# Two more 8 KB buffers for expert weights in a two-layer transformer block, and four kinds of small DMAs moved from GpSimd's queue to ScalarE's

## The chip, the cores and the metric

The kernel runs on one core of one Trainium2 chip. Its engines are TensorE (PE, with its weight loads as PEld), VectorE (DVE), ScalarE (ACT), GpSimd (POOL) and SyncE (SP); here SP does nothing but start DMAs, and ACT and POOL start a few as well. The metric is the device time of one execution in microseconds (us).

## The reference, cut to what matters

Two layers work on 256 latent tokens and 256 context tokens of 1024 features, all in float32. Each layer has a dense part and a mixture of experts. The second layer updates the latent tokens alone.

```python
for l in range(DEPTH):                                    # DEPTH = 2, last = (l == 1)
    mod_x = silu(c) @ w_mod[l] + b_mod[l]                 # six vectors: shift, scale and gate, twice
    mod_c = silu(c_ctx) @ w_mod[l] + b_mod[l]
    p_x = modulate(rmsnorm(x, norm1_g[l]), sh1, sc1) @ w_in[l]
    p_c = modulate(rmsnorm(ctx, norm1_g[l]), csh1, csc1) @ w_in[l]
    # attention, convolution and pooling branches, gated, merged, times w_out
    x = x + g1 * merge_branches(attn_x, conv_x, pool_x, gate_x, lp)
    if not last:
        ctx = ctx + cg1 * merge_branches(attn_c, conv_c, pool_c, gate_c, lp)
    x = x + g2 * expert_choice_ffn(modulate(rmsnorm(x, norm2_g[l]), sh2, sc2), ...)
    if not last:
        ctx = ctx + cg2 * expert_choice_ffn(modulate(rmsnorm(ctx, norm2_g[l]), csh2, csc2), ...)
return rmsnorm(x, final_norm_g)

def expert_choice_ffn(h, w_router, w_gate, w_up, w_down): # 16 experts, each takes its top 32 tokens
    aff = softmax(h @ w_router)
    g, idx = top_k(aff.T, 32)
    a, u = h[idx] @ w_gate[e], h[idx] @ w_up[e]           # w_gate, w_up, w_down: 1024 x 1024 per expert
    y[idx] += ((silu(a) * u) @ w_down[e]) * g
```

The three weight matrices of an expert have 4 MB each, so the experts of one layer read 192 MB, and of both layers 384 MB of the 530 MB that the kernel moves.

## The kernel before, in words

**Stages.** For each layer l the program runs through: the first norm with its modulation; the products for q, k and v; attention; the convolution and pooling branches; the merge of the branches; the output projection (`project`) with the router and its top 32 (`route`); the gather of the chosen tokens (`gather`); and a loop over 16 experts. Layer 0 works on both streams together (512 columns), layer 1 on the latent stream. In an expert, L1079 is the gate and up product, L1084 and L1086 the activation, L1094 the transposes, L1103 (layer 0) and L1108 (layer 1) the down product; L1115 and L1118 multiply by the gate, and after every fourth expert of layer 0, every second of layer 1, L1125 and L1128 add the group's result to the tokens.

**The dense weights.** w_mod, w_in and the like come in pieces of 512 KB or 1 MB into a ring of five buffers "w" of 8 KB per partition. SP starts these loads (L198, L363, L390, L728) in the order of the program, and each waits until the buffer that it is given is free.

**The start.** Nothing of layer 0 can begin before its first shift and scale are known. `mod_first` computes them in two halves of four feature blocks; each half takes eight loads of 512 KB from w_mod (L363), four buffers with two loads each, and multiplies them by the conditioning vectors (L367). Its bias is read from the small tiles mbias at L373. The four copies that fill mbias (L421: 64 partitions by 256, in which one row of b_mod is repeated over 32 partitions) are started by POOL before the change. Between the two halves SP starts two loads of w_in for q (L390). The transposes of the normed tokens (L404) and the first q products (L479, L480) stand between the halves on PE.

**The expert weights.** Each expert takes twelve loads of 1 MB: four pairs of gate and up, and four of down. `prefetch(n)` starts the next n loads on SP (L334), and `slot` says into which buffer each goes: it goes round a list, `order`, which names all buffers that are free by the time of the experts. In layer 0 the list has 15 entries (x0 to x3, the ring's five, two each of B and ws, A0, A1), and "y" once; in layer 1 it has 19. `eload` hands out a prefetched buffer and starts a new load where there is none. A load whose buffer is still read waits at the head of SP's queue, and everything behind it waits too.

**Small copies.** ACT already starts the biases of the later modulation products (modb, L227), the router's weights (rt, L839) and w_pool. Before the last expert POOL starts a copy of one row, final_norm_g (L1058), which PE spreads over the partitions (L1061).

**How order is made.** Each engine runs its instructions in the order that the program gives it, and waits on semaphores. DMAs started by SP or ACT use eight semaphores in turn, in the order of the program, over both queues; such a DMA waits until the one eight places before it has landed. DMAs started by POOL have semaphores of their own. DMAs that POOL starts have their descriptors built in on-chip memory, for which 16 KB per partition are set aside.

Of the kernel before, what the change touches and what calls it, by code (L numbers as in the profile page):

```python
# [10 lines left out]
F32 = mybir.dt.float32  # L11
# [7 lines left out]
DM, SEQ, CTX, DEPTH = 1024, 256, 256, 2  # L19
# [4 lines left out]
EPS = 1e-6  # L24
# per layer: conv taps issued per step of a section; engine of the low part of a split (v: DVE, p: GpSimd);
# engine that scales a head's probabilities; units per chunk of the modulation products
TAPS = dict(attn=(1, 4), pool=(4, 0), merge0=(8, 1), merge2=(9, 18))
# [11 lines left out]
def const_tables():  # L39
    """Tables that depend on shapes alone."""  # L40
    f = np.float32
    kc = np.zeros((128, KC_END), f)
    p = np.arange(128)
    kc[:, KC_ID:KC_ID + 128] = np.eye(128, dtype=f)
    kc[p ^ 16, KC_PERM + p] = 1.0
    kc[:, KC_U:KC_U + 128] = (p[:, None] <= p[None, :])
    kc[:, KC_MA:KC_MA + 128] = np.where(p[None, :] > p[:, None], f(-1e30), f(0))
    kc[:, KC_MB:KC_MB + 128] = np.where(p[None, :] < p[:, None], f(-1e30), f(0))
    kc[:, KC_IOTA:KC_IOTA + 32] = np.arange(1, 33)
    kc[:, KC_SCOL] = p % 32 + 1  # L50
    t = np.arange(SEQ)
    for g, w in enumerate(POOLW):
        cnt = np.clip(t + w - w // 2, 0, SEQ) - np.clip(t - w // 2, 0, SEQ)
        r = (f(w) / cnt.astype(f)).astype(f)
        kc[:, KC_EDGE + 16 * g:KC_EDGE + 16 * g + 8] = r[:8]
        kc[:, KC_EDGE + 16 * g + 8:KC_EDGE + 16 * g + 16] = r[-8:]
    row, col = (t // 64).astype(f), (t % 64).astype(f)
    fr = (f(10000.0) ** (-np.arange(16, dtype=f) / f(16))).astype(f)
    rope = np.zeros((128, 2, SEQ), f)
    for q in range(128):  # L60
        d = q % 64
        ang = (row if d < 32 else col) * fr[d % 16]
        sgn = f(-1.0) if (d // 16) % 2 == 0 else f(1.0)
        rope[q, 0] = np.cos(ang)
        rope[q, 1] = sgn * np.sin(ang)
    return kc, rope.reshape(128, 2 * SEQ)
# [3 lines left out]
def dit_block(ctx: ExitStack, tc: tile.TileContext, out, kc_in, rope_in, x, c, ctx_in, c_ctx,  # L70
# [3 lines left out]
    nc = tc.nc  # L74
# [9 lines left out]
    RB = 5  # L84
# [24 lines left out]

# [1 line left out]
    gps = open_psum("psd0", mm=3, md=1, ax=4)  # L111
# [11 lines left out]
    kt = misc[:, 512:512 + KC_END - KC_U]  # L123
# [7 lines left out]
    VN1, VN2, VCB, VLG, VLB, VPS = 0, 16, 32, 40, 48, 56  # L131
    nc.gpsimd.dma_start(kt, kc_in[:, KC_U:KC_END])

# [45 lines left out]
    def rms_scale(ss, n):  # L179
        """(ss / DM + EPS) ** -0.5"""  # L180
        r = small([128, 2], "rstd")
        nc.gpsimd.tensor_scalar(r[:, :n], ss[:, :n], 1.0 / DM, EPS, op0=ALU.mult, op1=ALU.add)
        nc.gpsimd.tensor_tensor(r[:, :n], r[:, :n], nhalf[:, :n], op=ALU.pow)
        return r

    for l in range(DEPTH):
        last = l == DEPTH - 1
        NS = 1 if last else 2
        N = 256 * NS

        # ================= dense part =================
        if l:
# [95 lines left out]

# [1 line left out]
        order = ["x0", "x1", "x2", "x3"]  # L290
        if last:
            order = ["xc", "A1"] + order + ["x4"] + ["w"] * RB + ["B", "B", "A0", "D", "D", "ws", "ws"]
        else:
            order += ["w"] * RB + ["B", "B", "A0", "A1", "ws", "ws"]
# [3 lines left out]
        def slot(name):  # L298
            if once and nload[0] == 4:
                tag = once.popleft()  # L300
            else:
                tag = order[nload[0] % len(order)]
                nload[0] += 1
            if tag == "w":
                return ring(name)
            if tag == "ws":
                return L.tile([128, 2048], F32, tag="ws", name=name, bufs=2)
            if tag == "xc":
                return P0.tile([128, 2048], F32, tag=tag, name=name)
            if tag[0] == "A":  # L310
                return half(tag, name)
            if tag in "BD":
                if tag in pair:
                    return pair.pop(tag)[:, 2048:]
                pair[tag] = big(tag, name)
                return pair[tag][:, :2048]
            return MO.tile([128, 2048], F32, tag=tag, name=name)
# [23 lines left out]

# [1 line left out]
        xn = [half(f"A{s}", "xn").rearrange("p (t d) -> p t d", t=2) for s in range(2)]  # L343
# [12 lines left out]
        def mod_first(hf, tag):  # L356
            """shift and scale of the first norm, feature blocks 4 hf .. 4 hf + 3"""
            ps = bank(tag)
# [57 lines left out]
        if l == 0:  # L416
            mbias = [t2("mbias", 256) for _ in range(2)]
            for f in range(2):
                for a in range(2):
                    o = 1024 * a + 512 * f  # L420
                    nc.gpsimd.dma_start(  # L421
                        mbias[f][64 * a:64 * a + 64], b_mod[0, o:o + 512].rearrange(
                            "(g n) -> g n", g=2).unsqueeze(1).to_broadcast([2, 32, 256]))
            first = mod_first(0, "md")
            next(first)
            small_operands()
            next(first, None)
            qw = [qload(0)]
            for d in range(4):
                modulated(d, (0, 1))  # L430
            for _ in mod_first(1, "ax"):
                pass
        else:
            qw = [qload(0)]
# [4 lines left out]
        def pump_mod(n=1):  # L439
            """advance the remaining modulation products by n chunks"""  # L440
            while n > 0:
                if cur_mod[0] is None:
                    if not bg:
                        return
                    cur_mod[0] = mod_group(*bg.popleft())
                if next(cur_mod[0], "end") == "end":
                    cur_mod[0] = None
                else:
                    n -= 1
# [25 lines left out]
        def mm3(ps, w, a, nk, n):  # L475
            """ps += w.T @ a over nk chunks of 128, each operand in two exact parts"""
            (wh, wl), (ah, al) = w, a
# [19 lines left out]

# [1 line left out]
        QS = DR.tile([128, NH, 256], F32R, tag="qf", name="QS")  # L499
# [17 lines left out]
        for u in range(2):  # L517
            tv = qw.pop() if qw else qload(u)
            for v in range(2):
# [5 lines left out]
                if NS == 2:  # L525
                    nc.scalar.activation(qx[:, 256:512], ps[:, 256:512], AF.Copy)
                # each head's rows: the leading part, and the rest on the other 64 partitions
                for kv in range(2):
# [28 lines left out]

# [1 line left out]
        def branch(name):  # L559
# [41 lines left out]
        def weigh(s, kv, pT, pr4, rs):  # L601
            """normalised probabilities, keys on the partitions"""
            nk = 4 if s == 0 else 2
# [31 lines left out]

# [1 line left out]
        W = 256 + 2 * CPAD  # L637
# [41 lines left out]

        if last:  # L680
            prefetch(2)

# [1 line left out]
        wp = DR.tile([128, 4, 128], F32, tag="k2", name="wp")  # L684
# [32 lines left out]

# [1 line left out]
        m = [half(f"A{i}", "m") for i in range(NS)]  # L719
# [46 lines left out]
        for g in range(4):  # L766
# [6 lines left out]
                                           op1=ALU.subtract)  # L773
# [1 line left out]
        def conv_norm():  # L775
# [51 lines left out]

        # ================= output projection, router, top-k =================
        tail[0] = True
# [55 lines left out]
        def route(s):  # L885
# [53 lines left out]
            wk = t2("wk", 256)  # L939
            m8 = MO.tile([48, 8], F32, tag="m8", name="m8", bufs=2)  # L940
            cur = pa[0:NE, 0:256]
# [36 lines left out]

# [1 line left out]
        def gather(s, parts):  # L980
# [17 lines left out]

        prefetch(2)
        rt = route(0)  # L1000
# [26 lines left out]

        # ================= experts =================
        GE = 4 if NS == 2 else 2
        REP = 128 // GE  # L1030
        nsq = [small([128, 2, 2], "nsq") for _ in range(NS)]
        for e in range(NE):
# [3 lines left out]
            if e % GE == GE - 1:  # L1036
                # scatter matrices of the group: (expert, slot) by token, scaled by the affinity
                sgs = []
# [16 lines left out]
            if last and e == NE - 1:  # L1055
                fgt, res = slot("fg"), slot("xo").rearrange("p (t d) -> p t d", t=2)
                frow, fg = fgt[0:1, 1024:2048], [fgt[:, 512 * h:512 * h + 512] for h in range(2)]
                nc.gpsimd.dma_start(frow, final_norm_g.unsqueeze(0))  # L1058
                for h in range(2):
# [4 lines left out]

            # gate and up: column tiles of the array side by side
            nb = 2 if NS == 2 else 1
# [136 lines left out]
```

## Time and profile before

| what | value |
|---|---|
| time, median of 3 runs (lowest to highest) | 1769.62 us (1764.06 to 1772.02) |
| span of the profiled execution, first to last instruction | 1765.2 us |
| mean granted TensorE clock | 0.953 of full speed |
| busy: PE, DVE, ACT, POOL | 87%, 38%, 23%, 13% |
| moved by DMA | 529.94 MB, mean 300 GB/s |
| layer 0: dense part and router, experts | 0 to 531 us, 531 to 1012 us |
| layer 1: dense part and router, experts and final norm | 1012 to 1297 us, 1297 to 1765 us |

The profiled execution has no time of its own on record besides its span, so sums are made against the span; the median of the three runs lies 4.4 us above it, which stands for what a run takes around its first and last instruction and for the scatter between runs. The busy shares are means over stages with different limits. In a stage in which the DMA engines move 409 GB/s all the time, PE's share says nothing about what bounds it; where PE is busy all the time and the DMA engines rest, the reverse holds.

### The profile page before, as it was taken

What the parts mean: (1) busy time and instruction counts of PE and PEld (TensorE: products, weight loads), DVE (VectorE), ACT (ScalarE), POOL (GpSimd) and SP (SyncE); (2) the same over time, 40 slices, a digit from 0 to 9 for tenths busy, and PEclk for the clock granted to TensorE, in tenths of its full rate; (3) what the DMA queues carried; (4) which work ended last, traced back from release to release, by engine and by line L of the source; (5) the groups of instructions that cost most, each with busy time, mean ns of one, the idle gap of its engine ahead of it and who ended that gap; (6) DMA issues with size and microseconds to landing.
All of it is one profiled execution on the core that took longest, in us unless ns stands there. A gap on an engine that the chain in (4) does not pass through costs nothing.

```text
span 1765.2 us, 19600 instructions
## 1 busy us (share of the span) xinstructions
PE 1537.8 (87%) x7792; PEld 809.1 (46%) x7792; DVE 668.7 (38%) x1144; ACT 407.7 (23%) x760; POOL 236.1 (13%) x242
## 2 busy tenths in 40 slices
PE   5999989999989999898899899999978766667676
PEld 2665566888654433232333267789742111111111
DVE  2568993452551221121211278965532110111011
ACT  2455312232431100000000157434421000000001
POOL 1300430154730000000000020225100000000000
PEclk9999999999999999999999999999989888888888
DMA  9733536254638999999999845666799999999996
GB/s 307 270 126 127 166 108 232 78 180 146 218 120 334 409 409 409 408 409 409 409 409 409 319 178 173 215 232 207 297 364 409 409 409 409 409 409 409 409 409 248
DMA packets 184331, 529.94 MB, mean 300 GB/s; under 512 B 11768, under 2 KB 60352, under 8 KB 179120
## 3 DMA queue, kind: packets, MB, share of 16 engines
q1 hardware_dynamic: 179472, 526.25, 78.4%
q10 hardware_dynamic: 4096, 1.97, 0.4%
q8 instruction: 61, 1.00, 0.2%
q0 software_dynamic: 672, 0.47, 0.1%
q14 instruction: 30, 0.25, 0.0%
HBM read 527.60 MB, written 1.05 MB: 299 GB/s over the span
## 4 chain that ended last, share of the span: by engine, by line
PE 37%; DMA 27%; DVE 5%; ACT 2%; POOL 2%; issue 1%; SPq 0%; POOLq 0%; ACTq 0%; DVEq 0%
DMA we<-in_w_e_up_dram 22%; PE mm L1079 11%; PE mm L1103 5%; DMA we<-in_w_e_down_dram 3%; PE mm L1108 3%; PE mm L480 2%; PE mm L988 2%; PE mm L479 2%; PE mm L482 2%; PE ax L1125 2%; PE mm L873 2%; DMA rt<-in_w_router_dram 1%; DVE hm L1086 1%; DVE acc L461 1%; PE ax L1094 1%
## 5 line engine op out<-in xcount | busy, mean ns | idle before, releaser
L1079 PE MATMUL mm<-we,xeT 128*64 128x512 f32 (+1 forms) x2048 | 445.9, 656 | 95.6 <-DMA we<-in_w_e_up_dram 75.3
L1079 PEld LDWEIGHTS mm<-we,xeT 128*64 128x64 f32 (+1 forms) x2048 | 126.6, 129 | 405.6 <-issue 201.1
L479 PE MATMUL mm<-hh,ws 128*128 128x512 f32 (+1 forms) x672 | 223.3, 351 | 1.4 <-ACT hh L413 1.2
L480 PE MATMUL mm<-hl,ws 128*128 128x512 f32 (+1 forms) x672 | 220.8, 347 | 0.0
L1086 DVE TENSOR_TENSOR hm<-si,mm 64x512 f32<-64x512 f32 x48 | 33.1, 690 | 468.1 <-ACT si L1084 467.2
L212 ACT ACTIVATE ws<-w 128x1024 fp32r<-128x1024 f32 x132 | 139.1, 1057 | 273.3 <-PE mm L482 186.2
L1084 ACT ACTIVATE si<-mm 64x512 f32<-64x512 f32 x48 | 28.4, 591 | 751.1 <-PE mm L1079 751.1
L461 DVE SCALAR_TENSOR_TENSOR acc<-up,dw,acc 128x512 f32<-128x512 f32 (+1 forms) x240 | 154.5, 687 | 0.9
L213 DVE TENSOR_TENSOR ws<-w,ws 128x1024 fp32r<-128x1024 f32 x94 | 123.6, 1319 | 71.9 <-ACT ws L212 71.5
L479 PEld LDWEIGHTS mm<-hh,ws 128*128 128x128 f32 x672 | 129.1, 193 | 31.5 <-issue 10.7
L480 PEld LDWEIGHTS mm<-hl,ws 128*128 128x128 f32 x672 | 129.2, 193 | 18.1 <-DVE hl L414 2.4
L1103 PE MATMUL mm<-we,hT 128*64 128x512 f32 x512 | 128.8, 635 | 8.4 <-ACT hT L1098 8.4
L482 PE MATMUL mm<-hh,ws 128*128 128x512 f32 (+1 forms) x672 | 134.8, 341 | 0.5 <-DVE ws L213 0.4
L213 POOL TENSOR_TENSOR ws<-w,ws 128x1024 fp32r<-128x1024 f32 x38 | 96.2, 2537 | 213.4 <-ACT ws L212 177.5
L482 PEld LDWEIGHTS mm<-hh,ws 128*128 128x128 f32 x672 | 107.6, 190 | 17.7 <-issue 2.4
L1044 POOL COPY sg<-kc 48x128 f32<-48x128 f32 (+1 forms) x16 | 4.4, 286 | 774.6 <-PE ax L1125 773.5
L1108 PE MATMUL mm<-we,hT 128*32 128x512 f32 x512 | 87.5, 790 | 11.9 <-DMA we<-in_w_e_down_dram 8.2
L1115 DVE TENSOR_TENSOR Y<-mm,G 32x512 f32<-32x512 f32 x64 | 44.0, 687 | 138.5 <-PE mm L1103 137.8
L1103 PEld LDWEIGHTS mm<-we,hT 128*64 128x64 f32 x512 | 39.2, 145 | 88.5 <-issue 75.1
L1125 PE MATMUL ax<-Y,sg 128*128 128x512 f32 x128 | 60.6, 619 | 8.8 <-DVE Y L1118 6.4
L1118 DVE TENSOR_TENSOR Y<-mm,G 64x512 f32<-64x512 f32 x32 | 22.0, 689 | 91.9 <-PE mm L1108 91.5
L749 POOL TENSOR_TENSOR m<-m,th 128x512 f32<-128x512 f32 (+1 forms) x32 | 36.6, 1143 | 145.1 <-DVE th L747 145.0
(271 smaller groups left out, 1594.6 us busy)
## 6 DMA issues: line engine op xcount, KB each, us to landing
we<-in_w_e_gate_dram SPq DMA_DIRECT2D x128, 1024.0 KB, 18.2
we<-in_w_e_up_dram SPq DMA_DIRECT2D x128, 1024.0 KB, 18.3
we<-in_w_e_down_dram SPq DMA_DIRECT2D x128, 1024.0 KB, 18.3
w<-in_w_mod_dram SPq DMA_DIRECT2D x40, 1024.0 KB, 5.0
w<-in_w_in_dram SPq DMA_DIRECT2D x38, 1024.0 KB, 5.2
w<-in_w_out_dram SPq DMA_DIRECT2D x12, 1024.0 KB, 5.1
w<-in_w_mod_dram SPq DMA_DIRECT2D x16, 512.0 KB, 10.8
w<-in_w_in_dram SPq DMA_DIRECT2D x8, 512.0 KB, 12.1
```

The source lines that it names most:

```text
L212: nc.scalar.activation(h, src, AF.Copy)
L213: (nc.gpsimd if eng == "p" else nc.vector).tensor_sub(lw, src, h.bitcast(F32))
L461: nc.vector.scalar_tensor_tensor(acc[:, ch], up[:, ch, :, k:k + 256], dw[:, 4 * k + ch:4 * k + ch + 1], acc[:, ch], op0=ALU.mult, op1=ALU.add)
L479: nc.tensor.matmul(ps, wh[:, k, :], ah[:, k, :n], start=k == 0, stop=False)
L480: nc.tensor.matmul(ps, wh[:, k, :], al[:, k, :n], start=False, stop=False)
L482: nc.tensor.matmul(ps, wl[:, k, :], ah[:, k, :n], start=False, stop=k == nk - 1)
L1079: nc.tensor.matmul(o, xeT[k // 4][:, k % 4, e, :], w[:, kk, 512 * f:512 * f + 512], start=k == 0, stop=k == 7)
L1086: nc.vector.tensor_mul(hm[0:64, :], si[0:64, :], pgu[f][64:128, :])
L1103: nc.tensor.matmul(pd[64 * h:64 * h + 64, :], hT[:, 64 * k:64 * k + 64], rhs, start=k == 0, stop=k == 7)
L1108: nc.tensor.matmul(pd[o:o + 32, :], hT[:, c0:c0 + 32], rhs, start=k < 2, stop=k >= 6)
L1115: nc.vector.tensor_mul(Y[b0:b0 + 32, s, cols], pd[rw, :], G2[l][rw, :])
L1125: nc.tensor.matmul(po, sgs[s][:, t * 128:(t + 1) * 128], Y[:, s, cols], start=True, stop=True)
```

## The change

Five things change, besides comments that are left out (line numbers from about L680 on are one lower in the new kernel, until L1188).

1. The 16 KB per partition for POOL's DMA descriptors are given up (64 bytes are left).
2. Two buffers e0 and e1 of 8 KB per partition take that room. They belong to the pool that lives through all phases, and stand ahead of x0 in `order`: 17 entries in layer 0, 21 in layer 1.
3. After attention both layers now prefetch: two loads in layer 0 (none before) and four in layer 1 (two before). The two loads that were prefetched ahead of the output projection stay in layer 1 only.
4. The DMAs that POOL started are started by ACT: the constants kt (L132), the four copies into mbias (L421), and the row of final_norm_g before the last expert (L1058).
5. The small tile m8 of the router's top-k has one buffer in place of two.

```diff
-    nc.gpsimd.dma_start(kt, kc_in[:, KC_U:KC_END])
+    nc.scalar.dma_start(kt, kc_in[:, KC_U:KC_END])
...
-        order = ["x0", "x1", "x2", "x3"]
+        order = ["x0", "x1", "x2", "x3"] if last else ["e0", "e1", "x0", "x1", "x2", "x3"]
         if last:
-            order = ["xc", "A1"] + order + ["x4"] + ["w"] * RB + ["B", "B", "A0", "D", "D", "ws", "ws"]
+            order = ["xc", "A1", "e0", "e1"] + order + ["x4"] + ["w"] * RB + ["B", "B", "A0", "D", "D", "ws", "ws"]
...
-            if once and nload[0] == 4:
+            if once and nload[0] == 6:
                 tag = once.popleft()
...
-            if tag[0] == "A":
+            if tag[0] in "Ae":
                 return half(tag, name)
...
-                    nc.gpsimd.dma_start(
+                    nc.scalar.dma_start(
                         mbias[f][64 * a:64 * a + 64], b_mod[0, o:o + 512].rearrange(
...
-        if last:
-            prefetch(2)
+        prefetch(4 if last else 2)
...
-            m8 = MO.tile([48, 8], F32, tag="m8", name="m8", bufs=2)
+            m8 = MO.tile([48, 8], F32, tag="m8", name="m8")
...
-        prefetch(2)
+        if last:
+            prefetch(2)
         rt = route(0)
...
-                nc.gpsimd.dma_start(frow, final_norm_g.unsqueeze(0))
+                nc.scalar.dma_start(frow, final_norm_g.unsqueeze(0))
...
-    nc = _bacc.Bacc("TRN2", target_bir_lowering=False, num_devices=1)
+    nc = _bacc.Bacc("TRN2", target_bir_lowering=False, num_devices=1,
+                    dynamic_dma_scratch_size=64)
```

**SP in the dense part of layer 0**, around the loads of modulation weights that run beside attention; "we" is a buffer for an expert's weights. Before:

```order
L198 DMA w<-in_w_mod_dram 128x2048 x2
L198 DMA w<-in_w_in_dram 128x8x256 x2
L198 DMA w<-in_w_mod_dram 128x2048 x3
L198 DMA w<-in_w_in_dram 128x8x256 x2
L198 DMA w<-in_w_mod_dram 128x2048 x4
```

After the change:

```order
L198 DMA w<-in_w_mod_dram 128x2048 x2
L198 DMA w<-in_w_in_dram 128x8x256 x2
L198 DMA w<-in_w_mod_dram 128x2048
L334 DMA we<-in_w_e_gate_dram 128x2x1024
L334 DMA we<-in_w_e_up_dram 128x2x1024
L198 DMA w<-in_w_mod_dram 128x2048 x2
L198 DMA w<-in_w_in_dram 128x8x256 x2
L198 DMA w<-in_w_mod_dram 128x2048 x4
```

Two loads of expert weights now stand between the first and the second of three loads of w_mod, about 83 us after the start. Every later load of expert weights in layer 0 is two numbers further on. In layer 1 the same place (about 1038 us) had one such load, and has three.

**SP at the start, with what each row waits for** (DMAHW0 to 7 are the eight semaphores; the rows shown end with the second half of `mod_first`). Before:

```order
L363 DMA w<-in_w_mod_dram 128x2x512 [waits DMAHW3_49]
L363 DMA w<-in_w_mod_dram 128x2x512 [waits DMAHW4_49]
L390 DMA w<-in_w_in_dram 128x8x128 [waits DMAHW5_49]
L390 DMA w<-in_w_in_dram 128x8x128 [waits DMAHW6_49]
L363 DMA w<-in_w_mod_dram 128x2x512 [waits DMAHW7_49,PE_49]
L363 DMA w<-in_w_mod_dram 128x2x512 [waits DMAHW0_49]
```

After the change:

```order
L363 DMA w<-in_w_mod_dram 128x2x512 [waits DMAHW0_49]
L363 DMA w<-in_w_mod_dram 128x2x512 [waits DMAHW1_49]
L390 DMA w<-in_w_in_dram 128x8x128 [waits DMAHW2_49]
L390 DMA w<-in_w_in_dram 128x8x128 [waits DMAHW3_49]
L363 DMA w<-in_w_mod_dram 128x2x512 [waits DMAHW4_49,PE_49]
L363 DMA w<-in_w_mod_dram 128x2x512 [waits DMAHW5_49]
```

The first two rows are the seventh and eighth load of the first half. Each waited for a load of SP's own; now the seventh, both loads of L390 and the first of the second half wait on the semaphores of the first, second, third and fourth copy into mbias.

**ACT at the start.** Before:

```order
L350 ACTIVATE junk,ss<-xr 128x1024 x2
L350 ACTIVATE junk,ss<-xc 128x1024 x2
L408 ACTIVATE hf<-ax,modT_99,A_0_101 128x256
L212 ACTIVATE ws<-w 128x1024 x2
L413 ACTIVATE hh<-hf 128x512
```

After the change:

```order
L350 ACTIVATE junk,ss<-xr 128x1024 x2
L350 ACTIVATE junk,ss<-xc 128x1024 x2
L421 DMA mbias<-in_b_mod_dram 64x1x256 x4
L408 ACTIVATE hf<-ax,modT_99,A_0_101 128x256
L212 ACTIVATE ws<-w 128x1024 x2
L413 ACTIVATE hh<-hf 128x512
```

The four copies stand behind the squares of the tokens (L350), the last of which waits for the context tokens.

## Rows read from the trace of the kernel before

**Rows 1.** The page's chain that ended last, shares of the span by line.

```profile
DMA we<-in_w_e_up_dram 22%; PE mm L1079 11%; PE mm L1103 5%; DMA we<-in_w_e_down_dram 3%; PE mm L1108 3%; PE mm L480 2%; PE mm L988 2%; PE mm L479 2%; PE mm L482 2%; PE ax L1125 2%; PE mm L873 2%; DMA rt<-in_w_router_dram 1%; DVE hm L1086 1%; DVE acc L461 1%; PE ax L1094 1%
```

**Rows 2.** Three stretches: engines' busy us, granted clock, DMA share, GB/s.

```profile
516.00:535.00 19.00, 17.47 (x83) 9.15 (x82) 11.64 (x38) 6.88 (x17) 0.00 (x0) 1.00 0.01 5
600.00:980.00 380.00, 348.26 (x1414) 124.96 (x1414) 72.46 (x110) 25.79 (x48) 1.58 (x6) 0.98 1.03 409
1310.00:1740.00 430.00, 311.86 (x1635) 77.11 (x1634) 56.81 (x89) 22.11 (x47) 2.61 (x8) 0.87 1.03 409
```

**Rows 3.** SP's timeline at the experts' start in both layers: start, duration, row.

```profile
508.84 0.37 SPq L334 DMA_DIRECT2D we<-in_w_e_up_dram  x1
535.15 0.37 SPq L334 DMA_DIRECT2D we<-in_w_e_gate_dram  x1
...
1278.42 3.01 SPq L334 DMA_DIRECT2D we<-in_w_e_gate_dram  x1
1299.55 0.37 SPq L334 DMA_DIRECT2D we<-in_w_e_up_dram  x1
```

**Rows 4.** SP's waits from 500 to 560 us: total, times, longest.

```profile
SPq L334 <- PE mm L1079: 34.0, 4, 26.0
```

**Rows 5.** SP's timeline, the same load of two experts that follow each other.

```profile
1688.36 2.30 SPq L334 DMA_DIRECT2D we<-in_w_e_up_dram  x1
...
1719.14 2.29 SPq L334 DMA_DIRECT2D we<-in_w_e_up_dram  x1
```

**Rows 6.** The chain in order of time, layer 0: start, duration, what.

```profile
684.39 19.84 DMA we<-in_w_e_up_dram
```

**Rows 7.** Two stretches of the dense parts, columns as in rows 2.

```profile
80.00:90.00 10.00, 10.00 (x51) 6.44 (x49) 4.71 (x8) 4.56 (x8) 2.46 (x3) 1.00 0.75 246
1050.00:1060.00 10.00, 9.05 (x52) 6.58 (x51) 8.08 (x16) 6.26 (x12) 1.23 (x1) 1.00 0.10 29
```

**Rows 8.** PE's waits from 20 to 460 us that name a DMA.

```profile
PE md L367 <- DMA w<-in_w_mod_dram: 5.2, 6, 2.6
```

**Rows 9.** The page's DMA issues: count, KB each, median us to landing.

```profile
w<-in_w_mod_dram SPq DMA_DIRECT2D x40, 1024.0 KB, 5.0
...
modb<-in_b_mod_dram ACTq DMA_DIRECT2D x20, 64.0 KB, 2.0
...
mbias<-in_b_mod_dram POOLq DMA_DIRECT2D x4, 64.0 KB, 9.4
```

**Rows 10.** ACT's timeline at the start, the end of L350.

```profile
13.82 0.19 ACT L350 ACTIVATION_READ_ACCUMULATOR junk<-xc 128x1 f32 x1
```

**Rows 11.** SP's timeline at the start: sixth and seventh load, second half's first.

```profile
11.24 1.65 SPq L363 DMA_DIRECT2D w<-in_w_mod_dram  x2
...
24.41 3.55 SPq L363 DMA_DIRECT2D w<-in_w_mod_dram  x1
```

**Rows 12.** Two stretches of the start, columns as in rows 2.

```profile
16.00:22.00 6.00, 2.48 (x20) 0.40 (x16) 1.26 (x2) 0.00 (x0) 0.00 (x0) 1.00 1.10 258
22.00:26.00 4.00, 2.69 (x24) 0.60 (x24) 0.00 (x0) 0.00 (x0) 0.00 (x0) 1.00 1.04 366
```

**Rows 13.** PE's timeline: first half's last two loads, second half's last three.

```profile
26.83 1.08 PE L367 MATMUL md<-w,cst 128*32 128x256 f32 x8 [0.28 <-DMA w<-in_w_mod_dram]
28.22 1.08 PE L367 MATMUL md<-w,cst 128*32 128x256 f32 x8 [0.31 <-DMA w<-in_w_mod_dram]
...
44.31 1.50 PE L367 MATMUL ax<-w,cst 128*32 128x256 f32 x24
```

**Rows 14.** Who waited for the router's weights, copied by ACT's queue.

```profile
  POOL rt L842: 15.1, 1
```

**Rows 15.** ACT's and PE's timelines near the end.

```profile
1711.53 0.39 ACT L1049 ACTIVATE af<-ax 128x256 f32<-128x256 f32 x1 [0.61 <-PE ax L1047]
...
1715.83 1.98 PE L1061 MATMUL ax<-fg,kc 1*128 1x512 f32 x4
...
1737.34 1.92 PE L1079 MATMUL mm<-we,xeT 128*32 128x512 f32 x14 [1.09 <-DMA we<-in_w_e_up_dram]
```

## The prediction

> **What bounds the kernel now.** I read the chain that ended last first, since it says which waits set the end. Its largest share is DMA of expert weights, 22% for the up loads and 3% for the down loads [rows 1]. The stretches show where that share lies. While layer 0 and layer 1 run their experts the DMA engines move 409 GB/s at a share of 1.03, and PE has room: it is busy 348 of 380 us in the one and 312 of 430 us in the other [rows 2]. In the chain put in order of time, the first long wait for an up load of layer 0 stands at 684 us [rows 6]: until there PE works off the loads that were waiting for it, and from there on it waits for each one. So the end of each expert stage is set by a stream of loads, and by when that stream starts.
>
> SP's timeline shows the start. In layer 0 all 15 buffers are full once the load issued at 508.84 has landed; the next one goes out at 535.15 [rows 3]. SP waits 26.0 us in that gap for the first gate product, L1079, to give a buffer back [rows 4], and from 516 to 535 us the DMA engines move 5 GB/s [rows 2]. Layer 1 has the same gap, 1278.42 to 1299.55 [rows 3]. What is in a buffer before the gap need not be loaded behind it. The dense parts are the reverse: PE is busy 10.0 of 10 us from 80 to 90 us, while the DMA share is 0.75 there, and 0.10 from 1050 to 1060 us [rows 7]. The only DMA that PE waits for between 20 and 460 us is w_mod in L367, right at the start [rows 8].
>
> **The expert buffers: what they remove.** Two more loads per layer fit ahead of the gap, so the stream behind it is two loads shorter. From the up load issued at 1688.36 to that of the next expert at 1719.14 are 30.78 us for twelve loads, 2.565 us each [rows 5]. Two loads in each of two layers: 4 x 2.565 = 10.26 us less. For this to arrive whole, the stream must start as before, at the first L1079. That product hangs on the dense part, the router and the gather, whose instructions the change leaves alone.
>
> **The expert buffers: what they add.** The four loads move into the dense parts, at about 83 us and 1038 us. There they lie ahead of w_mod loads. Two loads are 5.1 us of the DMA engines; at a share of 0.75 ten us leave 2.5 us free, the rest has to go into the stretches behind, and in layer 1 the emptiest stretch starts twelve us later with 9 of 10 us free [rows 7]. PE works on products already loaded meanwhile and has no DMA wait there to lengthen [rows 8]. I take nothing; the bound above is that two loads delay the dense chain by their own 5.1 us in one layer, which takes that layer's gain back. I take the lower end, as no wait for a dense load stands in the trace. The load into x1 now waits for the last step of the convolution branch, since x1 lies elsewhere; it fills buffers well ahead of the gap of 26.0 us [rows 4], and costs nothing unless it comes later than that. m8 is written and read by DVE alone, so one buffer adds no wait between engines: nothing. The 16 KB cost no time as such.
>
> **The copies at the start: what they move.** This is the part on which the size turns. POOL's four mbias copies need 9.4 us each [rows 9], beside loads of SP; nobody on SP waits for them. Now they stand on ACT behind L350, which ends at 14.0 (13.82 + 0.19) [rows 10], and they take four of the eight semaphores. The seventh w_mod load of the first half waits for copy 1, the two loads for q for copies 2 and 3, and the first load of the second half for copy 4. SP issues in order, so everything behind these waits too.
>
> First half. The seventh load went out behind one issued at 11.24, both done by 12.89 [rows 11]. Take POOL's time for a copy: 14.0 + 9.4 = 23.4 us until copy 1 lands. A load of w_mod then needs 5.0 us [rows 9] (the row of the 1 MB loads, the nearest without a long queue), so it lands at 28.4, and the eighth one step later. The steps between two loads' products are 28.22 - 26.83 = 1.39 us [rows 13], so 29.8 instead of 28.22: 1.6 us late. Queued behind the eighth load's product are the transposes and the first q products, then the second half; no wait for a DMA of theirs is on PE's list beside L367 [rows 8], so I let the 1.6 us go through to 45.81, where the second half's products end (44.31 + 1.50) [rows 13]. Second half: copy 4 is issued some 1.5 us after copy 1 and would land at 24.9, where its load went out at 24.41 before [rows 11]; that load's data are used much later (the last three loads' products start at 44.31 and wait for no DMA [rows 13]). So + 1.6 us in all.
>
> Bounds. From below: copies of the same 64 KB which ACT starts in a quieter place, modb, land in 2.0 us [rows 9]. Then copy 1 is there at 16.0, well before the six loads ahead are through, and nothing is late. There is even a gain to be had: from 16 to 22 us, as POOL's copies run, the DMA engines move 258 GB/s, and right after 366 [rows 12]. Without that dip (366 - 258) x 6 / 366 = 1.8 us come back, - 1.8. From above: the router's weights, 64 KB on ACT's queue behind expert loads, kept POOL waiting 15.1 us [rows 14]. Copy 1 at 29.1, its load at 34.1, the eighth at 35.5: + 7.3. I take 1.6, from the row of the very same copies in the same place, near the middle.
>
> The Trainium skill, DMA: Bandwidth & Descriptors, section "Why a DMA increments its semaphore by 16 and not by 1", speaks against this move: a DMA from SP's or ACT's queue runs on the largest number of DMA engines, up to 16, that divides the slowest dimension of both sides. A copy of mbias reads 2 rows, repeated, into 64 partitions, so by that page two DMA engines would carry each copy, and the four copies would queue on the same two. No row here shows engines one by one; by the page alone the copies would come one behind the other, which is rival E's order, and the sum would be E's if each took as long as on POOL.
>
> **The other copies.** kt goes out on ACT at the start, in place of POOL, and 192 KB early on hide behind the token loads: nothing. The row of final_norm_g goes out on ACT behind L1049, at 1711.9, where PE wants it at 1715.83 [rows 15]. With 2.0 to 9.4 us it lands between 1713.9 and 1721.3. At worst PE stands 5.5 us, but PE waits for up loads until 1737.34 [rows 15] anyway; SP's last up load (1719.14 [rows 5]) waits for it too, at worst 2.2 us, under loads that are already queued. Nothing, as long as the queue holds.
>
> **Sum.** 1765.2 - 10.26 + 1.6 = 1756.5 us of span. The median of the runs shown is 4.4 us above the span, so against it 1769.6 - 8.7 = 1761.0 us, or 0.49% less.
>
> **The rivals.**
>
> A is the forecast, 1761.0.
>
> B, the start gets shorter: the copies on ACT's queue land as fast as modb. For it speaks that row, against it that SP's queue is full at that time. 1765.2 - 10.26 - 1.8 = 1753.1, against the median 1757.5.
>
> C, one layer's gain is given back: the two loads collide with dense loads there, or the start of the stream shifts. For it speaks the DMA share of 0.75 at 80 us, against it that PE waits for no dense load. 1765.2 - 5.13 + 1.6 = 1761.7, against the median 1766.1.
>
> D, the buffers do nothing: what sets the end of a stage is not the loads but PE. For it speaks that PE is busy 348 of 380 us in layer 0, against it the chain from 684 us on. 1765.2 + 1.6 = 1766.8, against the median 1771.2.
>
> E, on the other side: the copies land one behind the other, and SP's loads stand behind the last. At 9.4 us each copy 4 lands at 14.0 + 4 x 9.4 = 51.6; the first load of the second half is there 5.0 us later and the other seven at 1.39 us each, 66.3 in place of 44.31, + 22.0. 1765.2 - 10.26 + 22.0 = 1776.9, against the median 1781.3. It decides once copy 4 lands after 44.31 + 10.26 - 14.7 = 39.9, that is when the copies come more than 5.5 us apart. Against it: POOL's four copies all had that time side by side, and copies that find the loads stalled should be quicker.
>
> **How the numbers follow.** A 42%, B 22%, C 16%, D 10%, E 10%. About 0.5%, 8.8 us, is what a measurement of this kernel can tell from no change, and A lies on that bound. The start may cost less than 1.6 us sooner than more, since modb's row is one of the very queue that the copies now take, so of A's 42 I count 26 beyond the bound and 16 within. Faster: 22 + 26 = 48%. Within: 16 + 16 + 10 = 42%. Slower: 10%. A, B and C make 80%; the range reaches from 2 us under B to 2 us over C, 1755.5 to 1768 us.
>
> **What would show it.** Right: the gap of SP before the experts has the same end relative to the first L1079 but the stream behind has two loads less, and the first L1079 of each layer comes at the same distance from the layer's start; four loads at 83 and 1038 us; the first half's last L367 at 29.8 in place of 28.22; copy 1 landing near 23 us and SP's seventh load right behind it. Wrong: PE waits for w_mod or w_in after 80 or 1038 us (C); a step from L1079 to L1079 in layer 0's last experts that is not 30.8 us (D); SP idle from 25 to 40 us, and L367 waiting for DMA in the second half (E); 366 GB/s from 16 to 22 us (B); PE L1061 with a long wait for fg.

## The result, and the profile after

The changed kernel takes 1757.63 us (median of 4 runs, 1754.98 to 1759.45) against 1767.67 us before (median of 4, 1764.06 to 1772.02). The ratio is 0.9948, with a 95% interval of 0.9933 to 0.9964. The profiled execution took 1757.78 us with a span of 1756.0 us, where 1756.5 was forecast.

The stretches that answer to [rows 2] show two streams that run as before, at 409 GB/s (columns as there; in layer 1 it is 409 GB/s from 1310 to 1720 us too):

```profile
605.00:985.00 380.00, 349.25 (x1430) 124.61 (x1428) 72.99 (x112) 26.74 (x50) 1.58 (x6) 0.99 1.03 409
...
1306.00:1336.00 30.00, 29.47 (x228) 14.02 (x231) 9.97 (x18) 5.28 (x12) 0.29 (x1) 1.00 1.03 410
```

The page's rows on the chain, by engine and by line (shares of the span):

```profile
DMA 20%; PE 15%; DVE 3%; ACT 1%; issue 1%; POOL 1%; POOLq 0%; ACTq 0%; DVEq 0%; SPq 0%
DMA we<-in_w_e_up_dram 13%; DMA we<-in_w_e_down_dram 6%; PE mm L1079 3%; PE mm L480 2%; PE mm L482 2%; PE mm L479 2%; PE mm L1108 1%; PE mm L987 1%; DMA rt<-in_w_router_dram 1%; DVE acc L461 1%; DVE ws L213 1%; PE ax L628 1%; PE md L233 1%; PE mm L872 0%; PE ax L1125 0%
```

This time the chain could be followed through 41% of the span only, so its shares don't compare with [rows 1]; its order does, since the expert weights lead again. What can be compared is when the stream of each layer starts and ends. SP's timeline after the change, the two new loads of layer 0 and the rows that answer to [rows 3] (start, duration, row):

```profile
84.48 0.34 SPq L198 DMA_DIRECT2D w<-in_w_mod_dram  x1
84.87 0.43 SPq L334 DMA_DIRECT2D we<-in_w_e_gate_dram  x1
85.35 0.46 SPq L334 DMA_DIRECT2D we<-in_w_e_up_dram  x1
...
512.29 0.37 SPq L334 DMA_DIRECT2D we<-in_w_e_up_dram  x1
540.23 0.37 SPq L334 DMA_DIRECT2D we<-in_w_e_gate_dram  x1
...
1296.26 1.41 SPq L334 DMA_DIRECT2D we<-in_w_e_down_dram  x2
```

PE's timeline after the change, the first gate product of layer 0, the last wait for an up load of layer 0, and the same two of layer 1:

```profile
536.55 13.95 PE L1079 MATMUL mm<-we,xeT 128*64 128x512 f32 x64
...
981.03 3.65 PE L1079 MATMUL mm<-we,xeT 128*64 128x512 f32 x12 [0.64 <-DMA we<-in_w_e_up_dram]
...
1294.29 7.07 PE L1079 MATMUL mm<-we,xeT 128*32 128x512 f32 x64
...
1728.99 2.37 PE L1079 MATMUL mm<-we,xeT 128*32 128x512 f32 x11 [1.51 <-DMA we<-in_w_e_up_dram]
```

Before, the same four stood at 531.47, 982.16, 1297.58 and 1737.34 (the last in [rows 15]):

```profile
531.47 13.95 PE L1079 MATMUL mm<-we,xeT 128*64 128x512 f32 x64
...
982.16 3.65 PE L1079 MATMUL mm<-we,xeT 128*64 128x512 f32 x12 [0.64 <-DMA we<-in_w_e_up_dram]
...
1297.58 3.64 PE L1079 MATMUL mm<-we,xeT 128*32 128x512 f32 x32
```

So layer 0's stage from the first product to the last wait got shorter from 450.69 to 444.48 us, - 6.2, and layer 1's from 439.76 to 434.70, - 5.1. But layer 0's experts start 5.1 us later than before. The places where that time went are at the start and, as the windows below show, in PE's clock.

The start, PE's timeline, to be set beside [rows 13]: the first half's last two loads and the second half's last three.

```profile
29.12 1.08 PE L367 MATMUL md<-w,cst 128*32 128x256 f32 x8 [4.03 <-DMA w<-in_w_mod_dram]
30.82 1.08 PE L367 MATMUL md<-w,cst 128*32 128x256 f32 x8 [0.62 <-DMA w<-in_w_mod_dram]
...
45.74 1.50 PE L367 MATMUL ax<-w,cst 128*32 128x256 f32 x24
```

The second half's products, by the same matmuls, come 45.74 - 44.31 = 1.43 us later than before. PE waits 4.03 us for the seventh load. SP's timeline says why: the seventh load, the two for q, and the first of the second half.

```profile
21.95 0.37 SPq L363 DMA_DIRECT2D w<-in_w_mod_dram  x1
24.69 0.37 SPq L390 DMA_DIRECT2D w<-in_w_in_dram  x1
26.63 0.37 SPq L390 DMA_DIRECT2D w<-in_w_in_dram  x1
30.21 0.37 SPq L363 DMA_DIRECT2D w<-in_w_mod_dram  x1
```

These are the four loads that wait for mbias copies 1 to 4, which ACT issued from 13.34 us on. They go out 2.7, 1.9 and 3.6 us apart: the copies come one behind the other, and SP stands in between. The trace's record of single packets shows the copies themselves: in ACT's queue each ends with two packets of 4 bytes, at 20.4 and 21.5, 23.5 and 24.1, 24.9 and 25.8, 27.8 and 29.6 us, and each of the four loads goes out 0.5 to 0.8 us behind the second packet of its copy. The windows of the start show the price, DMA engines that rest while a 64 KB copy is waited for (columns as in [rows 2]):

```profile
16.00:20.00 4.00, 2.50 (x20) 0.41 (x16) 1.00 (x2) 0.00 (x0) 0.00 (x0) 1.00 1.00 352
20.00:24.00 4.00, 2.16 (x16) 0.40 (x16) 0.00 (x0) 0.00 (x0) 0.00 (x0) 1.00 0.44 125
24.00:30.00 6.00, 1.96 (x16) 0.40 (x16) 0.00 (x0) 0.00 (x0) 0.00 (x0) 1.00 1.06 310
30.00:32.00 2.00, 1.28 (x12) 0.20 (x8) 0.00 (x0) 0.00 (x0) 0.00 (x0) 1.00 0.58 125
```

Beside POOL's copies the DMA engines moved 258 GB/s from 16 to 22 us [rows 12]; now they move 352 from 16 to 20 us, and 125 in two stretches behind.

From 46 to 490 us the distance of the two traces, taken over VectorE's instructions one by one, stays between 1.3 and 2.2 us, and it is 1.9 at the end. Two places then add 1.6 us each, and in both the work is the same and the granted clock is not:

```profile
490.50:493.80 3.30, 3.30 (x9) 2.57 (x8) 3.06 (x12) 0.00 (x0) 1.61 (x1) 0.50 0.13 14
...
531.20:536.50 5.30, 5.30 (x32) 5.22 (x32) 2.34 (x9) 3.27 (x10) 0.00 (x0) 0.68 0.00 0
```

For 3.3 us from 490.5 on the granted clock is 0.50, the lower of the two levels (1.2 GHz), while PE is busy all the time. PE had been busy 2.84 of 5.00 us from 485 to 490, and 1.82 of 3.00 us from 528 to 531.

### The profile page after: what moved, and what is told of

It is laid out like the page before. It is cut to its first block, busy times and chain, and to the rows that moved or that the text cites. A ratio compares the mean times of both kernels' runs of the same rounds, so it can differ in the third digit from the quotient of the medians.

```text
span 1756.0 us, 19578 instructions
## 1 busy us (share of the span) xinstructions
PE 1521.9 (87%) x7792; PEld 806.1 (46%) x7792; DVE 669.9 (38%) x1144; ACT 408.2 (23%) x760; POOL 230.3 (13%) x236
## 5 line engine op out<-in xcount | busy, mean ns | idle before, releaser
L1079 PE MATMUL mm<-we,xeT 128*64 128x512 f32 (+1 forms) x2048 | 442.9, 644 | 91.8 <-DMA we<-in_w_e_up_dram 71.4
L1079 PEld LDWEIGHTS mm<-we,xeT 128*64 128x64 f32 (+1 forms) x2048 | 125.0, 127 | 402.0 <-issue 198.9
L1103 PE MATMUL mm<-we,hT 128*64 128x512 f32 x512 | 122.2, 610 | 8.4 <-ACT hT L1098 8.4
L1108 PE MATMUL mm<-we,hT 128*32 128x512 f32 x512 | 81.7, 732 | 20.8 <-DMA we<-in_w_e_down_dram 16.9
```

What stands on the lines that cost most here:

```text
L1079: nc.tensor.matmul(o, xeT[k // 4][:, k % 4, e, :], w[:, kk, 512 * f:512 * f + 512], start=k == 0, stop=k == 7)
L1103: nc.tensor.matmul(pd[64 * h:64 * h + 64, :], hT[:, 64 * k:64 * k + 64], rhs, start=k == 0, stop=k == 7)
L1108: nc.tensor.matmul(pd[o:o + 32, :], hT[:, c0:c0 + 32], rhs, start=k < 2, stop=k >= 6)
```

## The experiments

Each kernel was compared with the kernel before on the chip on which it ran. All edits are against the changed kernel.

**The moved DMAs alone.**

```diff
-        order = ["x0", "x1", "x2", "x3"] if last else ["e0", "e1", "x0", "x1", "x2", "x3"]
+        order = ["x0", "x1", "x2", "x3"]
         if last:
-            order = ["xc", "A1", "e0", "e1"] + order + ["x4"] + ["w"] * RB + ["B", "B", "A0", "D", "D", "ws", "ws"]
+            order = ["xc", "A1"] + order + ["x4"] + ["w"] * RB + ["B", "B", "A0", "D", "D", "ws", "ws"]
...
-            if once and nload[0] == 6:
+            if once and nload[0] == 4:
...
-        prefetch(4 if last else 2)
+        if last:
+            prefetch(2)
...
-        if last:
-            prefetch(2)
+        prefetch(2)
```

The third place is the prefetch after attention, the fourth the one ahead of the output projection.

> The changed kernel without e0 and e1: the DMAs stay on ACT's queue, the buffers and prefetches are those of before. If the whole gain comes from loads that need not stand behind the gap ahead of the experts, this kernel has none of it and keeps the cost of the start, 1.4 us in the profile after: 1.0008 of the time before, between 1.000 and 1.002. At the start the DMA engines should run below 150 GB/s from 20 to 24 us, and the first half's last L367 should stand near 30.8 as in the profile after. Rival, the moved copies bring part of the gain (POOL's four copies hold up the DMA engines from 16 to 22 us): 0.999 or less, and that L367 before 28.2.

Measured: 1770.56 us against 1765.45, ratio 1.0034 (1.0022 to 1.0046), + 5 us and outside the 1.000 to 1.002 expected. The last L367 of the second half stands at 48.08, 3.8 us late. About 1.5 of these are not the copies: from 41.00 to 44.40 us this trace has a granted clock of 0.50, and PE's steps there take 1.5 us longer than in the profile after. A second such stretch (491.6 to 495.0, 0.50) brings the first L1079 to 5.3 us behind the one before. So in this trace some 2.3 us are the start and 3.1 the clock; whether the other four runs, 5 to 8 us over, had the same stays open, since the trace is of one. The rival, a gain from the copies, is out. Whether another of the moved DMAs costs too is asked again in the square (below).

**e0 and e1 in layer 1 alone** (layer 0's list and prefetch as in the kernel before).

> The changed kernel with e0 and e1 used in layer 1 alone; layer 0 has 15 buffers and no prefetch after attention, as before. If each layer gives 2 x 2.565 = 5.13 us, layer 0's share is lost: 1.4 - 5.1 = - 3.7 us, 0.998 of the time before. Rival, layer 0 gives nothing since its experts start some 5 us later in the profile after: the ratio stays near 0.995. Second rival, layer 1 gives nothing: 1.0008.

Measured: 1763.95 us against 1765.45, ratio 0.9994 (0.9984 to 1.0004): only 1 us faster, where 3.7 were expected. The stage lengths are as expected, 450.7 us in layer 0 and 434.6 in layer 1 (table below). In the one trace the start is 2.6 us late, of which about 1.5 fall in a stretch with a granted clock of 0.50 (38.7 to 42.1 us), and a second such stretch (530.2 to 533.6) adds 1.6. That this makes up the miss in all twelve runs is not shown. Neither rival holds: layer 1 has its 5 us, and layer 0's are missing.

**Two buffers less than before.**

```diff
-        order = ["x0", "x1", "x2", "x3"]
+        order = ["x0", "x1"]
```

(on top of the first experiment's edit)

> No e0 and e1, and in both layers also without x2 and x3: two buffers less than before, with the DMAs on ACT. If a buffer is worth 2.565 us per layer also on this side, 4 x 2.565 + 1.4 = 11.7 us more, 1.0066 of the time before. Rival, fewer buffers open holes in the stream: well over 1.0066, and below 409 GB/s in the middle of an expert stage. Second rival, the number does not matter: 1.0008.

Measured: 1777.05 us against 1765.45, ratio 1.0071 (1.0059 to 1.0083), as the sum has it. Set beside the first experiment on the same chip, though, it is 6.5 us more and not 10.3. In the two traces the stages account for 9.7 us (table below), and the first experiment's trace gives back 3.9 ahead of the experts, by its later start and its stretches at the lower clock; so the two times alone don't show what a buffer is worth. From 605 to 975 us it moves the same 409 GB/s, so no holes:

```profile
605.00:975.00 370.00, 336.41 (x1352) 117.58 (x1349) 71.52 (x108) 23.72 (x43) 1.58 (x6) 1.00 1.03 409
```

**Wide copies.** The same 64 KB in four copies, cut so that each fills 32 partitions.

```diff
-            mbias = [t2("mbias", 256) for _ in range(2)]
-            for f in range(2):
-                for a in range(2):
-                    o = 1024 * a + 512 * f
-                    nc.scalar.dma_start(
-                        mbias[f][64 * a:64 * a + 64], b_mod[0, o:o + 512].rearrange(
-                            "(g n) -> g n", g=2).unsqueeze(1).to_broadcast([2, 32, 256]))
+            mb = t2("mbias").rearrange("p (f n) -> p f n", f=2)
+            mbias = [mb[:, f, :] for f in range(2)]
+            for a in range(2):
+                for g in range(2):
+                    o = 1024 * a + 256 * g
+                    nc.scalar.dma_start(
+                        mb[64 * a + 32 * g:64 * a + 32 * g + 32], b_mod[0, o:o + 1024].rearrange(
+                            "(f n) -> f n", f=2)[:, 0:256].unsqueeze(0).to_broadcast([32, 2, 256]))
```

> The changed kernel with the four mbias copies cut otherwise: each fills 32 partitions of both halves from two pieces of 256 (32 x 512, 64 KB as before, in the form that modb's copies have), in place of 64 partitions of one half from two rows. If the narrow form is why copies 1 to 4 came at 22, 24.7, 26.6 and 30.2 us (the times at which SP's waiting loads went out), these land within about 4 us of their issue, SP's seventh load goes out before 19 us, no stretch from 16 to 28 us falls below 300 GB/s, and the first half's last L367 stands at or before 28.2: 1.4 to 3.5 us less than the changed kernel, 0.993 to 0.994 of the time before. The Trainium skill, DMA: Bandwidth & Descriptors, section on why a DMA increments its semaphore by 16, would have the first form run on two DMA engines and this one on sixteen. Rival, it is the place in the turn of eight semaphores, behind SP's full queue, that makes them late: the same issue times as in the profile after, and 0.995.

Measured: 1752.3 us against 1765.45, ratio 0.9931 (0.9919 to 0.9943). Its SP timeline, the seventh load, the first for q, and the first of the second half:

```profile
18.81 0.37 SPq L363 DMA_DIRECT2D w<-in_w_mod_dram  x1
...
20.66 0.47 SPq L390 DMA_DIRECT2D w<-in_w_in_dram  x1
...
23.95 3.30 SPq L363 DMA_DIRECT2D w<-in_w_mod_dram  x1
```

Its windows at the start, with the hole gone:

```profile
16.00:20.00 4.00, 2.16 (x16) 0.43 (x16) 0.45 (x1) 0.00 (x0) 0.00 (x0) 1.00 1.08 333
20.00:24.00 4.00, 2.78 (x24) 0.60 (x24) 0.00 (x0) 0.00 (x0) 0.00 (x0) 1.00 1.04 381
...
30.00:32.00 2.00, 2.00 (x12) 1.98 (x11) 1.94 (x9) 0.00 (x0) 0.00 (x0) 1.00 1.05 388
```

And PE's last products of the second half, 2.0 us ahead of before:

```profile
42.33 1.50 PE L367 MATMUL ax<-w,cst 128*32 128x256 f32 x24
```

The first of the second half no longer waits for a copy but 2.0 us for PE (L367) to give back its buffer. The page's row of ACT's queue (packets, MB, share), changed kernel and then wide:

```profile
q10 hardware_dynamic: 4506, 2.43, 0.5%
```

```profile
q10 hardware_dynamic: 4562, 2.43, 0.5%
```

The 56 packets more are all of 4 bytes: in the trace's record of packets the four copies have 256 packets of 1 KB in both kernels, and behind each narrow copy stand two packets of 4 bytes, behind each wide one sixteen. The last of them comes at 20.5 us, against 29.6 with narrow copies. Two of the signs expected were missed: the wide copies landed 6.6 us (median) behind their issue, not about 4, and from 18 to 20 us the DMA engines moved 279 GB/s.

Same bytes, same queue, same semaphores, packets of the same size: the form of the copies is the cause. The rival, their place in the turn of the semaphores, predicted unchanged issue times and falls.

**The square.** Buffers or none, narrow or wide, the four on one chip. The corner with no buffers and wide copies joins the edits of the first and the fourth experiment.

> Four kernels make a square on one chip: e0 and e1 or not, mbias copies narrow (64 x 256) or wide (32 x 512). This one is the changed kernel as it is: buffers, narrow. In the runs so far it stood 9 us under before and the kernel without the buffers 5 us over, 14 us apart, where the sum of loads gives 10.3. If the sum of loads holds, this kernel is 10.3 us under the one with narrow copies and no buffers, within some 2 us. Rival, the buffers are worth more than their loads, since with more of them other holes close: 13 us or more.

> The square's corner with no buffers and narrow copies: the cost of the moved DMAs alone, measured again. The traces so far show the second half's last L367 1.3 to 3.8 us later than before; the time was 5 us over before. If the start is all, 1 to 4 us over before; rival, another of the moved DMAs (kt, the final norm's row) costs as well: 5 us again, and a lag that grows behind 50 us or at the end.

> The square's corner with no buffers and wide copies: about 2 us under before, as the start of the kernel with wide copies was 2.0 us ahead of before. By the sum of loads it is 10.3 us over the corner with wide copies and buffers; the rival, buffers worth more, has 13 or more.

> The square's corner with buffers and wide copies, measured again: 12 us under before, and 3.4 to 6 us under the changed kernel (first-half and second-half lag of + 1.3 to + 3.8 us against - 2.0 us). If narrow copies cost no more than the start, both rows of the square show the same difference between the columns.

Measured, all against 1767.62 us before:

| | no buffers | e0 and e1 | difference |
|---|---|---|---|
| narrow | 1768.32 us, 1.0005 (0.9996 to 1.0015) | 1758.21 us, 0.9944 (0.9929 to 0.9960) | 10.1 us |
| wide | 1765.07 us, 0.9989 (0.9979 to 0.9999) | 1753.81 us, 0.9923 (0.9908 to 0.9937) | 11.3 us |
| difference | 3.3 us | 4.4 us | |

The buffers are worth 10 to 11 us in both rows, which is the sum of loads; the rival of 13 or more falls. The moved DMAs alone cost 0.7 us here and 5 us in the first run of the same kernel on another chip; in this trace the lag is 1.2 us at 45 us and 0.8 to 1.6 from there to the experts of layer 1, and 2.0 at their end, where layer 1's stage is 0.9 us longer than before. So up to there nothing but the start is charged. That the same kernel stands 5 us over before in one set of runs and 0.7 in the other, with intervals that don't overlap, is more than the intervals allow for. The stretches at the lower clock explain one trace of it; the rest is open. Differences of a few us are compared here within one chip, as in the square, and by stage lengths.

**Earlier copies.** The four copies, narrow or wide, issued by ACT right behind kt.

> The changed kernel with the four narrow mbias copies issued by ACT right behind kt, ahead of the squares, at about 2 to 4 us in place of 13 to 15.6. If what costs the start is only that SP's loads wait for copies that come late, these land long before the seventh load, and the second half's last L367 stands at 40 to 43 as with wide copies: 3 to 4 us under the changed kernel, 0.992 to 0.993 of the time before. Rival, the narrow form costs wherever it stands, since the copies hold up the token loads on the engines that they use: the last token load and the first w_mod load come later by as much as is won, 0.994 to 0.995.

> As before this one, with wide copies. If the two remedies do the same thing, the time is that of wide copies behind the squares: 0.992 to 0.993 of the time before, last L367 of the second half at 40 to 42. If each takes a part of its own, 0.990 to 0.991.

Measured against 1766.11 us: narrow and early 1755.61 us, 0.9939 (0.9922 to 0.9957); wide and early 1752.02 us, 0.9918 (0.9906 to 0.9931). The time of narrow and early overlaps both expectations; its trace decides for the rival. PE's first products of `mod_first` (L367 in the other kernels), narrow and then wide:

```profile
19.78 1.08 PE L374 MATMUL md<-w,cst 128*32 128x256 f32 x8 [6.29 <-DMA w<-in_w_mod_dram]
```

```profile
16.64 1.08 PE L375 MATMUL md<-w,cst 128*32 128x256 f32 x8 [5.23 <-DMA w<-in_w_mod_dram]
```

And the windows from 10 to 16 us, narrow and then wide:

```profile
10.00:16.00 6.00, 0.34 (x1) 0.18 (x1) 1.55 (x3) 1.57 (x3) 0.89 (x2) 1.00 0.53 149
```

```profile
10.00:16.00 6.00, 0.34 (x1) 0.18 (x1) 1.55 (x3) 3.00 (x6) 0.97 (x3) 1.00 0.86 291
```

Issued early, the narrow copies stand in the way of the token loads and of the first w_mod loads. They do it through SP's queue: SP waits 4.3 us for mbias copies there, the last of which lands at 12.2 us, and starts the context tokens' loads at 11.71, against 9.86 with wide ones. The second half's last products come at 44.49, against 42.01 with wide ones, whose trace has a granted clock of 0.51 from 33.5 to 36.9 us, worth about 1.4 us. In these traces early alone takes 1.2 us off the changed kernel's 45.74, wide alone 3.4, and both together 3.7; but the second trace with wide copies behind the squares has 40.08, so whether early issue adds anything to the wide form is not shown. Wide copies, behind the squares or early, make the fastest kernels of the study, 0.992 to 0.993 of the time before, faster than both kernels of the case.

## Why the prediction was right, step by step

**The streams (10.26 us less).** The stage lengths of all kernels, from the first L1079 to the last wait of the same row, in us:

| buffers, layer 0 / layer 1 | kernels | layer 0 | layer 1 |
|---|---|---|---|
| 13 / 17 | fewer | 456.0 | 444.9 |
| 15 / 19 | before, moved (two runs), wide without buffers | 450.7 to 451.6 | 439.6 to 440.7 |
| 15 / 21 | layer 1 alone | 450.7 | 434.6 |
| 17 / 21 | changed (two runs), wide (two runs), early (two) | 444.5 to 445.2 | 434.7 to 435.7 |

By the means of these rows two buffers are worth 4.9 (the first pair) and 6.2 us (the second) in layer 0, and 5.0 and 5.0 us in layer 1, where two loads at 2.565 us are 5.13 [rows 5]. It holds in both directions and in each layer by itself, whatever the copies do, so this step is shown. In layer 0 the second pair gives 1 us more than its loads; about half of that is a hole behind the restart that 17 buffers fill. From 20 to 40 us behind the first L1079 the DMA engines move 381 to 391 GB/s in the five traces with 15 buffers and 392 to 399 in the six with 17; ten GB/s more over 20 us are 0.2 MB, or 0.5 us at 409 GB/s. The other half stays open.

**What the loads add to the dense parts (nothing).** From the last L367 to the first L1079 it takes 487.2 us before and 486.8 to 490.8 in the other kernels: with e0 and e1 in layer 0 it is 487.1 to 487.3 in five traces of six, without them 486.8 to 489.1. In layer 1 it takes 311.6 to 313.9 us from the last wait of layer 0's experts to the first L1079 with e0 and e1, and 312.7 to 315.4 without. No trace shows rival C's collision, in either layer, and in the profile after PE waits for no dense load from 60 to 480 us or from 1020 to 1270. The 490.8 of the profile after hold its two clock dips.

**The start (+ 1.6 us).** Measured + 1.43 in the profile after, and 1.2 to 3.8 over six traces with narrow copies in their first place; the two above 1.6 hold a stretch at the lower clock and would stand near 2.3 and 1.1 without it. The sum's size was right, the route was not the one described, and that the size fits is in part luck. The seventh load did wait for copy 1, until 21.95 (23.4 was worked out). It then took 7.2 us from its issue to its product at 29.12, where 5.0 were taken, and the first half was 2.6 us late instead of 1.6. The step that failed is that copy 4 would land at 24.9 because the four run side by side. They came one behind the other, as rival E has it, with copy 4's last packet at 29.6 and SP's load behind it at 30.2; but at 1.9 to 3.6 us apart, under the 5.5 from which E decides (5.5 counts from copy 1 at 23.4), and no L367 of the second half waits for a DMA. The prediction let the first half's delay through in full; the trace let 1.4 of 2.6 us through. The Trainium skill, DMA: Bandwidth & Descriptors, section "Why a DMA increments its semaphore by 16 and not by 1", would have the narrow copies share two DMA engines and the wide ones use all sixteen. The trace agrees in the count: two packets of 4 bytes end each narrow copy and sixteen each wide one. The wide copies' last packet at 20.5 us in place of 29.6 agrees as well; which engines they were, no row shows.

Rival B, that the start gets shorter, was not what this change does, but it is what it would do with copies in the wide form: - 2.0 to - 4.2 us in the four traces with them. Its reason, copies as fast as modb's 2.0 us, did not hold even there: the wide copies took 6.6.

**The other copies (nothing).** kt, the shared tile m8 and the room given up have no run of their own; all three are in the kernel with narrow copies and no buffers, which is 0.7 us over before in the square with a start 1.2 us late. The row of final_norm_g was issued at 1704.81, and PE's L1061 waited for it a little, as the row shows, while waits for up loads follow:

```profile
1709.15 1.98 PE L1061 MATMUL ax<-fg,kc 1*128 1x512 f32 x4 [0.47 <-DMA fg<-in_final_norm_g_dram]
...
1718.76 1.92 PE L1079 MATMUL mm<-we,xeT 128*32 128x512 f32 x14 [1.50 <-DMA we<-in_w_e_up_dram]
```

**The sum.** Forecast 8.7 us less, measured 9.2 by the ratio and 9.4 in the square's corner. As a time, 1761.0 us was forecast and 1757.63 measured: of the 4.4 us that were put on top of the span, the profiled run of the changed kernel shows 1.8, and the rest was scatter of three runs. Part of the agreement of the two spans is luck: of the 9.2 us between them, layer 0's experts start 5.1 us late, where 1.6 was forecast, and 6.2, 2.2, 5.1 and 0.9 us come off in layer 0's stage, between the two stages, in layer 1's stage and behind its last wait. Layer 0's extra 1 us and the clock dips shown below, at different places of the two traces, partly cancel: 1.6 of the 2.2 us are a dip of the trace before.

## What to carry to other kernels

Where a stage is bound by a stream of loads that starts from full buffers, a buffer is worth about one load's time on the stream per stage (2.4 to 3.1 us here, where a load takes 2.565); count it from the issue times of one period, and look in the gap ahead of the stage whether the loads have room. When a DMA changes its queue, ask who will wait on its semaphore, and in what form it moves its bytes: four 64 KB copies cost 3 to 4 us here by their access pattern alone, a third of what two buffers of 8 KB gave.

## What the hardware showed that was not expected

PE's granted clock falls to the lower level (0.50) in short stretches. Some stand in every trace (near 235 us), others come at places that change from run to run, and each of these costs 1.5 to 1.6 us where PE sets the pace. In the profile after it did so at 490.5 (granted 0.50) and in the gather at 531.2 (0.68 over 5.3 us). The same kernel's second trace had neither. In the kernel before it fell at the end of layer 0's experts, 6 us after PE's last wait for an up load, and the distance of the two traces shifts by 1.6 us there:

```profile
985.00:995.00 10.00, 8.37 (x22) 2.71 (x21) 1.38 (x2) 1.76 (x3) 0.00 (x0) 0.83 1.04 336
```

PE's busy time ahead of it does not tell the cases apart, and what does stays open: without a dip, the kernel with narrow copies and no buffers had PE busy 2.83 of 5.00 us from 485 to 490, against 2.84 in the profile after. A difference of 1.6 us between two single traces is therefore no evidence by itself; stage lengths over several traces are.
